# Pinning the spill operations in the gate and up products, and separate buffers for the block sums of the down product

## The chip, the cores and the metric

The kernel runs on one core of one Trainium2 chip. The metric is the time of one execution on the device, in microseconds (us). Engines are named as in the profile: PE is TensorE (PEld its weight load), DVE is VectorE, ACT is ScalarE, POOL is GpSimd, SP is SyncE, which issues most DMAs (SPq is its queue).

## The reference

One step of a streaming encoder layer: RMSNorm, an input projection, two groups of attention heads, an output projection, then the feed-forward part, in which the change lies, and a final RMSNorm.

```
h = rmsnorm(x, lp['norm_ffn_g'])
x = x + (jax.nn.silu(h @ lp['ffn_w_gate']) * (h @ lp['ffn_w_up'])) @ lp['ffn_w_down']
```

There are 576 tokens that are kept (512 prompt and 64 sample), the model width is 2048, the inner width 5632. All data are float32.

## The kernel before

**How a product is made.** The feed-forward part multiplies by blocks in the Winograd form of Strassen's scheme. A weight block of two row tiles by two column tiles has quarters a11, a12, a21, a22; seven products p1 to p7 replace eight. The left operands are p1 = a11, p2 = a12, p4 = a22, p5 = a21 + a22, p6 = (p5's sum) - a11, p3 = a12 - (p6's), p7 = a11 - a21. The tokens, two halves of 288, take the place of the right operand's columns; their combinations are made once and reused.

`winograd` (line 1153) does this for one column block of 256 weights. Its inner function `lhs` (line 1178) makes the left operand of a product: POOL forms p5's sum in a tile `ws` (line 1186) and p7's difference in place in the weights' tile `raw` (line 1195); DVE forms p6's difference in place in `ws` (line 1189) and p3's in place in `raw` (line 1192). `split_weights` then splits the float32 operand in two: ACT copies it, rounded, into `wh` (line 156), and DVE subtracts to get the rest, `wl` (line 153). I call this pair a split. `wh` and `wl` have two buffers each, so the split for one product can be made when PE is done with that of the product before the last. PE multiplies `wh` by both parts of the tokens (line 1207) and then `wl` by the large part (line 1211). `take` then moves the result out of PSUM: in the gate and up products ACT copies (line 1300) and DVE adds (line 1303), in the down product DVE adds into `y` (line 1472). Several products share a PSUM bank and pile up in it; the next one may not start before `take` has read the last.

**Gate and up.** 22 rounds, u = 0 to 21. Each round runs the seven products for the gate weights (I call this a gate set), then the seven for the up weights (an up set), in the order 1, 2, 4, 5, 6, 3, 7. The contraction has 8 steps, so a product is 16 matmuls with `wh` and 8 with `wl`. Behind the gate set `gated` (line 1360) applies the norm's factor on DVE, silu on ACT and the factor again on POOL. Behind the up set POOL multiplies the two (line 1429, two halves) and forms four combinations of the result (lines 1434 to 1437), the right operands of the down product.

**The spill.** These operands don't fit on the chip, so `spill_operands` (line 1340) writes them to memory. It handles two parts of four slices (from u = 20 on one part). Per slice, ACT copies the rounded value to a tile `s` (line 1345) and DVE subtracts it in place from the slice in the tile `c` (line 1346); after four slices two stores of 576 KB go out, and the next part needs the tile `s`, of which there is one, again. The generator is advanced by `step`, which `winograd` calls after each product of the next round: before the change from the second to the sixth product of the gate set and after each of the up set; what is left is run out at the end of the round.

**Who sets the order.** The kernel is written as one program for all engines, and a scheduler orders each engine's instructions. It places an instruction where it takes it to be ready. PE's matmuls are in the order of the program. What the spill does on ACT and DVE may float: the scheduler puts it where it judges the operands to be there. An engine runs its queue in order, so an instruction that waits holds back all behind it.

**Down.** 5632 inner rows are taken in blocks of 4, 4, 4, 4, 4 and 2 pairs of row tiles. For each of the first five blocks there are eight rows of the loop over d (line 1563), each a `winograd` call for 256 output columns (`down_rows`, line 1465) with 4 contraction steps: 8 matmuls with `wh` and 4 with `wl` in a product. I call each of the 40 calls a down row; its products come in the order 1, 5, 6, 2, 7, 3, 4. `raw` has two buffers here, and the weights of a row are loaded by SP when the row before the last has let go of its buffer. The last user of a `raw` is the split of p4. The very first down row still runs beside the spill of u = 21. The block of 2 is multiplied without the scheme (`plain_rows`, line 1445), and `finish` (line 1492) writes the outputs.

`raw` for the first two down rows is loaded by DMAs that POOL issues (line 1402).

Of the kernel before, what the change touches and what calls it, by code (L numbers as in the profile page):

```python
# [19 lines left out]
P = 128  # L20
# [95 lines left out]
def encoder_step(  # L116
# [1034 lines left out]
        return pm.tile([P, 512], F32, name="m", tag="m")  # L1151

    def winograd(wpool, spool, raws, slots, take, banks=None, engine=V, step=lambda: None, stag=("ws", 1),
                 chain=(), made=None):

        first, last = not banks, take is not None
        banks = {} if banks is None else banks

        def split_weights(n, srcs):
            wh = wpool.tile([P, n, P], F32R, name="wh", tag="wh", bufs=2)
            wl = wpool.tile([P, n, P], F32R, name="wl", tag="wl", bufs=2)
            k = 0
            for s in srcs:
                split(wh[:, k:k + s.shape[1], :], wl[:, k:k + s.shape[1], :], s)
                k += s.shape[1]  # L1170
            return wh, wl

        vs = [r.rearrange("p (m t) (f c) -> p t f m c", t=2, f=2) for r in raws]
        n = sum(v.shape[3] for v in vs)
        a11, a12, a21, a22 = ([v[:, t, f] for v in vs] for f in range(2) for t in range(2))
        sums = []

        def lhs(p):
            if made and p in made:
                return made[p]  # L1180
            if p == 5:
                w = spool.tile([P, n, P], F32, name="ws", tag=stag[0], bufs=stag[1])
                ends = np.cumsum([0] + [x.shape[1] for x in a21]).tolist()
                sums.extend(w[:, a:b, :] for a, b in zip(ends, ends[1:]))
                for x, y, z in zip(sums, a21, a22):
                    G.tensor_tensor(x, y, z, op=ALU.add)  # L1186
            elif p == 6:
                for x, y in zip(sums, a11):
                    engine.tensor_tensor(x, x, y, op=ALU.subtract)  # L1189
            elif p == 3:  # L1190
                for x, y in zip(sums, a12):
                    V.tensor_tensor(y, y, x, op=ALU.subtract)
            elif p == 7:
                for x, y in zip(a11, a21):
                    G.tensor_tensor(y, x, y, op=ALU.subtract)  # L1195
            return split_weights(n, {1: a11, 2: a12, 4: a22, 5: sums, 6: sums, 3: a12, 7: a21}[p])

        shared = {}
        for p, name in chain or [(p, p) for p in ORDER]:
            new = name not in shared  # L1200
            if first:
                shared[name] = banks[p] = shared[name] if not new else pmt()[:, 0:QH]
            wh, wl = lhs(p)
            for k in range(n):
                hi, lo = operands[slots[k], p]
                for x in (hi, lo):
                    PE.matmul(banks[p], wh[:, k, :], x, start=first and new and k == 0 and x is hi, stop=False,  # L1207
                              skip_group_check=not new)
            for k in range(n):
                hi, lo = operands[slots[k], p]  # L1210
                PE.matmul(banks[p], wl[:, k, :], hi, start=False, stop=last and k == n - 1,  # L1211
                          skip_group_check=not new)
            if last:
                take(p, banks)
            step()
# [124 lines left out]
    def spill_operands(m, parts):  # L1340

        for first, src in parts:
            hi = squad(F32R)
            for k in range(4):
                S.activation(hi[:, k], src[:, k], AF.Copy)  # L1345
                V.tensor_tensor(src[:, k].bitcast(F32R), src[:, k], f32(hi[:, k]), op=ALU.subtract)  # L1346
                yield
            store(opspill[m, :, first:first + 4, 0], f32(hi))
            store(opspill[m, :, first:first + 4, 1], src)
            yield  # L1350
# [36 lines left out]
    for u in range(FC // 2):  # L1387
        out = {}
        for which, wsrc in (("g", w_gate), ("u", w_up)):
            first = turn == 0  # L1390
            now = raw[:, 0:8] if first else raw
            if turn < FC - 1:
                raw = load_pair((fr, fb)[(turn + 1) % 2], (w_up, w_gate)[turn % 2], (turn + 1) // 2 * 256)
            turn += 1
            c = fc.tile([P, 2, TQ], F32, name="c", tag="c" + which, bufs=1 + (which == "g"))
            chain = () if first else CHAIN if u == FC // 2 - 1 and which == "u" else WIDE
            take = combined(*quarters(c[:, 0, :], c[:, 1, :]), chain)
            if u == FC // 2 - 1 and which == "u":
                raw = fr.tile([P, 16, 256], F32, name="raw", tag="raw", bufs=1)
                fetched = {(0, d): raw[:, 8 * d:8 * d + 8] for d in range(2)}  # L1400
                for d in range(2):
                    G.dma_start(fetched[0, d], w_down[0:1024, d * 256:d * 256 + 256].rearrange("(k p) c -> p k c", p=P))

            products = [0]

            def step():
                products[0] += 1
                if which == "u" or 1 < products[0] < 7:
                    next(spilling, None)
                if u == 0 and which == "u":  # L1410
                    next(norm, None)
                if u == FC // 2 - 1 and which == "u":
                    if products[0] == 2:
                        load_y(0)
                    for _ in range(blocks[0]):
                        next(start, None)

            if first:
                winograd(fw, rw, [now], range(4, 8), take, banks0, step=step)
            else:  # L1420
                winograd(fw, rw, [now], range(8), take, step=step, chain=chain)
            out[which] = c
            if u and which == "g":
                gated(c)
# [40 lines left out]
    def down_rows(m0, n, d, slots, step):  # L1465
        raws = [fetched.pop((m0, d))]
        y11, y12, y21, y22 = quarters(y[2 * d], y[2 * d + 1])
        parts = {1: (y11,), 5: (y22,), 6: (y12,), 2: (y11,), 7: (y22,), 3: (y12,), 4: (y21,)}

        def take(p, banks):  # L1470
            for c in parts[p]:
                V.tensor_tensor(c, c, banks[p], op=ALU.add)  # L1472

        spool, bufs = (yy, 2) if m0 + d else (rw, 1)
        winograd(fw, spool, raws, slots, take, step=step, stag=("ws", bufs), chain=CHAIN)

    tok = [[(0, NS), (NS, P), (192, 96)], [(QH, P), (416, P), (544, 32)]]
    sqs = {}
# [13 lines left out]
    def finish(h, ahead):  # L1492
# [27 lines left out]
        for i, (q, j) in enumerate(groups):  # L1520
            o, n = tok[h][j]
            ps = held.pop(0) if held else turned(q, j)
            tag, bufs = ("ws", 2) if i % 3 < 2 else ("ot", 1)
            ot = yy.tile([P, 4, P], F32, name="ot", tag=tag, bufs=bufs).rearrange("p a b -> p (a b)")
            if i % 2:
                S.activation(ot[0:n], ps[0:n, :], AF.Copy, scale=rc[0:n, j:j + 1])  # L1526
            else:
# [134 lines left out]
```

## Time and profile before

| what | value |
|---|---|
| time, three runs | 2471.19, 2474.02, 2477.39 us; median 2474.02 |
| the profiled execution's own time | 2474.84 us |
| its span | 2473.1 us |
| granted PE clock, mean | 0.995 |
| busy: PE, PEld | 2391.3 us (97%), 2343.1 us (95%) |
| busy: DVE, ACT, POOL | 1856.6 (75%), 1133.8 (46%), 817.1 us (33%) |
| DMA | 353.03 MB, mean 143 GB/s |

The profiled execution took 1.7 us more than its span. Gate and up run from about 907 us to 1915 us of the span, the 40 down rows from there to 2387 us, the rest to the end.

How to read it: a row of a timeline gives the start, the time from the first to the last end of the instructions merged in the row, the engine, line and operation, output and inputs, the count, and in brackets how long the engine stood idle before and what let it go. `PE L1207 ... x16` is the first part of a gate or up product, `L1211 ... x8` its second; in the down rows these are x8 and x4. Ends of matmuls are modelled, so the starts of products tell more than idle times.

### The profile page before, as it was taken

How to read it: one execution, taken by the hardware profiler on the slowest of the kernel's cores; microseconds unless marked ns; L12 is line 12 of the kernel's file. 1: busy time of each engine (PE TensorE's matmuls, PEld its weight loads, DVE VectorE, ACT ScalarE, POOL GpSimd, SP SyncE). 2: the span in 40 equal slices, each digit the busy share in tenths (PEclk: the TensorE clock that was granted, in tenths of full speed). 3: DMA queues.
4: the chain of work that ended last, by engine and by line, in shares of the span. 5: the costliest groups of instructions: out<-in, count | busy, mean ns of one | idle time of the engine just before them, and what ended most of it. 6: DMA issues, size and time to landing. Idle time of an engine off the chain costs nothing. (4 is left out here: it accounts for less than half of the span.)

```text
span 2473.1 us, 44094 instructions
## 1 busy us (share of the span) xinstructions
PE 2391.3 (97%) x17544; PEld 2343.1 (95%) x17544; DVE 1856.6 (75%) x2748; ACT 1133.8 (46%) x1977; POOL 817.1 (33%) x525
## 2 busy tenths in 40 slices
PE   7999999999999999999999999999999999999997
PEld 7999999999998998999999999999999999999986
DVE  5666676666664788778778788787787888888875
ACT  5445545334453554444444444444444333333345
POOL 1100000120000455555555655555554222222245
PEclk9999999999999999999999999999999999999999
DMA  7432233253323644344444444443546873563334
GB/s 223 142 96 83 83 98 94 66 156 102 99 82 118 185 152 146 113 163 151 134 152 141 142 151 134 157 158 113 170 151 212 301 243 125 198 220 108 102 103 145
DMA packets 361972, 353.03 MB, mean 143 GB/s; under 512 B 25087, under 2 KB 319637, under 8 KB 361765
## 3 DMA queue, kind: packets, MB, share of 16 engines
q1 hardware_dynamic: 359535, 343.43, 43.5%
q0 software_dynamic: 1904, 6.24, 0.8%
q8 instruction: 138, 2.26, 0.4%
q10 hardware_dynamic: 325, 0.53, 0.1%
q14 instruction: 70, 0.57, 0.1%
HBM read 271.68 MB, written 81.16 MB: 143 GB/s over the span
## 5 line engine op out<-in xcount | busy, mean ns | idle before, releaser
L1207 PE MATMUL m<-b,wh 128*128 128x288 f32 x7168 | 1050.1, 295 | 16.6 <-DVE y L1472 8.5
L1207 PEld LDWEIGHTS m<-b,wh 128*128 128x128 f32 x7168 | 982.8, 188 | 23.6 <-issue 16.7
L153 DVE TENSOR_TENSOR wl<-raw,wh 128x512 fp32r<-128x512 f32 (+1 forms) x457 | 600.3, 1314 | 59.3 <-ACT wh L156 59.0
L1211 PE MATMUL m<-b,wl 128*128 128x288 f32 x3584 | 583.4, 298 | 11.7 <-DVE wl L153 11.5
L156 ACT ACTIVATE wh<-raw 128x512 fp32r<-128x512 f32 (+1 forms) x457 | 380.1, 832 | 410.3 <-PE m L1207 275.1
L1211 PEld LDWEIGHTS m<-b,wl 128*128 128x128 f32 x3584 | 512.4, 188 | 21.5 <-DVE wl L153 21.5
L1186 POOL TENSOR_TENSOR ws<-raw 128x1024 f32<-128x1024 f32 (+1 forms) x85 | 201.7, 2373 | 619.3 <-DVE wl L153 289.7
L156 ACT ACTIVATE wh<-ws 128x512 fp32r<-128x512 f32 (+1 forms) x170 | 144.2, 848 | 222.3 <-DVE ws L1189 180.0
L108 PE MATMUL ps<-xh,wh 128*128 128x296 f32 x992 | 225.9, 309 | 0.1
L108 PE MATMUL ps<-xl,wh 128*128 128x296 f32 x992 | 217.7, 301 | 0.3 <-DVE xl L161 0.3
L108 PE MATMUL ps<-xh,wl 128*128 128x296 f32 x992 | 216.9, 300 | 0.0
L1195 POOL TENSOR_TENSOR raw<-raw 128x1024 f32<-128x1024 f32 (+1 forms) x85 | 207.1, 2437 | 6.6
L153 DVE TENSOR_TENSOR wl<-ws,wh 128x512 fp32r<-128x512 f32 (+1 forms) x170 | 164.5, 968 | 17.5 <-ACT wh L156 17.4
L1346 DVE TENSOR_TENSOR c<-c,s 128x288 fp32r<-128x288 f32 x168 | 84.6, 533 | 110.6 <-POOL c L1437 59.7
L108 PEld LDWEIGHTS ps<-xh,wh 128*128 128x128 f32 x992 | 161.6, 191 | 3.7 <-issue 0.6
L108 PEld LDWEIGHTS ps<-xl,wh 128*128 128x128 f32 x992 | 162.3, 190 | 1.0 <-DVE xl L161 0.9
L108 PEld LDWEIGHTS ps<-xh,wl 128*128 128x128 f32 x992 | 162.2, 190 | 0.0
L1472 DVE TENSOR_TENSOR y<-y,m 128x288 f32<-128x288 f32 x280 | 126.0, 450 | 46.1 <-PE m L1211 46.1
L153 DVE TENSOR_TENSOR wl<-wr,wh 128x1024 fp32r<-128x1024 f32 (+1 forms) x110 | 120.7, 1097 | 31.7 <-ACT wh L156 30.4
L156 ACT ACTIVATE wh<-wr 128x1024 fp32r<-128x1024 f32 (+1 forms) x110 | 102.2, 929 | 75.3 <-PE ps L108 50.7
L1345 ACT ACTIVATE s<-c 128x288 fp32r<-128x288 f32 x168 | 63.2, 434 | 151.9 <-POOL c L1429 130.6
L1429 POOL TENSOR_TENSOR c<-c 128x576 f32<-128x576 f32 x44 | 101.1, 2297 | 80.6 <-DVE c L1303 78.9
(370 smaller groups left out, 3194.7 us busy)
## 6 DMA issues: line engine op xcount, KB each, us to landing
raw<-in_ffn_w_gate SPq DMA_DIRECT2D x44, 1024.0 KB, 5.5
raw<-in_ffn_w_up SPq DMA_DIRECT2D x44, 1024.0 KB, 7.9
b<-opspill SPq DMA_DIRECT2D x148, 288.0 KB, 5.9
raw<-in_ffn_w_down SPq DMA_DIRECT2D x38, 1024.0 KB, 5.6
wr<-in_w_in SPq DMA_DIRECT2D x56, 512.0 KB, 4.1
opspill<-s SPq DMA_DIRECT2D x42, 576.0 KB, 3.1
opspill<-c SPq DMA_DIRECT2D x42, 576.0 KB, 3.1
wr<-in_w_out SPq DMA_DIRECT2D x16, 512.0 KB, 4.3
```

Source lines behind the costliest of these rows:

```text
L108: self.tc.keep_in_program_order(self.pe.matmul(out, lhsT, rhs, start=start, stop=stop))
L153: V.tensor_tensor(lo, src, f32(hi), op=ALU.subtract)
L156: S.activation(hi, src, AF.Copy)
L1186: G.tensor_tensor(x, y, z, op=ALU.add)
L1195: G.tensor_tensor(y, x, y, op=ALU.subtract)
L1207: PE.matmul(banks[p], wh[:, k, :], x, start=first and new and k == 0 and x is hi, stop=False, skip_group_check=not new)
L1211: PE.matmul(banks[p], wl[:, k, :], hi, start=False, stop=last and k == n - 1, skip_group_check=not new)
L1345: S.activation(hi[:, k], src[:, k], AF.Copy)
L1346: V.tensor_tensor(src[:, k].bitcast(F32R), src[:, k], f32(hi[:, k]), op=ALU.subtract)
L1429: G.tensor_tensor(w[:, f, :], w[:, f, :], g[:, f, :], op=ALU.mult)
L1472: V.tensor_tensor(c, c, banks[p], op=ALU.add)
```

## The change

Three things change.

1. The two spill operations are pinned: `keep_in_program_order` ties an instruction to the one traced just before it on the same engine, so that it can't be placed ahead of that one. It adds no wait. Other instructions may still float. `step` now advances the spill from the third product of a gate set and the second of an up set on.
2. `winograd` gets a switch `within`. For every down row but the first it is off: then p6's and p3's differences on DVE and p7's on POOL go to tiles `ws` of their own instead of being made in place. A row takes four such tiles from three buffers (before: one tile from two buffers). The output tiles of `finish` use the same three buffers, where they had these two and one of their own.
3. The first `raw` of the down product is loaded by SP instead of POOL.

```diff
-                 chain=(), made=None):
+                 chain=(), made=None, within=True):
...
-            if p == 5:
+            if p in (5, 6, 3, 7) and (p == 5 or not within):
                 w = spool.tile([P, n, P], F32, name="ws", tag=stag[0], bufs=stag[1])
                 ends = np.cumsum([0] + [x.shape[1] for x in a21]).tolist()
-                sums.extend(w[:, a:b, :] for a, b in zip(ends, ends[1:]))
-                for x, y, z in zip(sums, a21, a22):
-                    G.tensor_tensor(x, y, z, op=ALU.add)
-            elif p == 6:
-                for x, y in zip(sums, a11):
-                    engine.tensor_tensor(x, x, y, op=ALU.subtract)
-            elif p == 3:
-                for x, y in zip(sums, a12):
-                    V.tensor_tensor(y, y, x, op=ALU.subtract)
-            elif p == 7:
-                for x, y in zip(a11, a21):
-                    G.tensor_tensor(y, x, y, op=ALU.subtract)
-            return split_weights(n, {1: a11, 2: a12, 4: a22, 5: sums, 6: sums, 3: a12, 7: a21}[p])
+                new = [w[:, a:b, :] for a, b in zip(ends, ends[1:])]
+            else:
+                new = {6: sums, 3: a12, 7: a21}.get(p)
+            if p == 5:
+                sums.extend(new)
+            left, right = {5: (a21, a22), 6: (sums, a11), 3: (a12, sums), 7: (a11, a21)}.get(p, ((), ()))
+            for x, y, z in zip(new or (), left, right):
+                (G if p in (5, 7) else V).tensor_tensor(x, y, z, op=ALU.add if p == 5 else ALU.subtract)
+            if p == 6:
+                sums[:] = new
+            return split_weights(n, new or {1: a11, 2: a12, 4: a22}[p])
...
-                S.activation(hi[:, k], src[:, k], AF.Copy)
-                V.tensor_tensor(src[:, k].bitcast(F32R), src[:, k], f32(hi[:, k]), op=ALU.subtract)
+                tc.keep_in_program_order(S.activation(hi[:, k], src[:, k], AF.Copy))
+                tc.keep_in_program_order(
+                    V.tensor_tensor(src[:, k].bitcast(F32R), src[:, k], f32(hi[:, k]), op=ALU.subtract))
...
-                    G.dma_start(fetched[0, d], w_down[0:1024, d * 256:d * 256 + 256].rearrange("(k p) c -> p k c", p=P))
+                    load(fetched[0, d], w_down[0:1024, d * 256:d * 256 + 256].rearrange("(k p) c -> p k c", p=P))
...
-                if which == "u" or 1 < products[0] < 7:
+                if products[0] > (2, 1)[which == "u"]:
                     next(spilling, None)
...
-        spool, bufs = (yy, 2) if m0 + d else (rw, 1)
-        winograd(fw, spool, raws, slots, take, step=step, stag=("ws", bufs), chain=CHAIN)
+        spool, bufs = (yy, 3) if m0 + d else (rw, 1)
+        winograd(fw, spool, raws, slots, take, step=step, stag=("ws", bufs), chain=CHAIN, within=m0 + d == 0)
...
-            tag, bufs = ("ws", 2) if i % 3 < 2 else ("ot", 1)
-            ot = yy.tile([P, 4, P], F32, name="ot", tag=tag, bufs=bufs).rearrange("p a b -> p (a b)")
+            ot = yy.tile([P, 4, P], F32, name="ot", tag="ws", bufs=3).rearrange("p a b -> p (a b)")
```

What this does to the order is shown at two places; line numbers of the changed kernel are one or two smaller from `lhs` on.

The first place is DVE at the border of an up set and the next gate set, in the steady part of gate and up. `wl<-raw` and `wl<-ws` are the second half of a split, `c<-c,m` adds of `take`, `c<-c,s` the spill's subtraction. Before:

```order
L1303 TENSOR_TENSOR c<-c,m 128x288
L153 TENSOR_TENSOR wl<-raw,wh 128x1024
L1346 TENSOR_TENSOR c<-c,s 128x288
L1303 TENSOR_TENSOR c<-c,m 128x288 x2
L153 TENSOR_TENSOR wl<-raw,wh 128x1024
L1346 TENSOR_TENSOR c<-c,s 128x288 x3
L153 TENSOR_TENSOR wl<-raw,wh 128x1024
L1303 TENSOR_TENSOR c<-c,m 128x288
L153 TENSOR_TENSOR wl<-ws,wh 128x1024
```

The three `wl<-raw` are those of the gate set's p1, p2 and p4: one spill subtraction stood ahead of p2's, three ahead of p4's.

The same place now, from p1's `wl` of the gate set on:

```order
L153 TENSOR_TENSOR wl<-raw,wh 128x1024
L1301 TENSOR_TENSOR c<-c,m 128x288 x2
L153 TENSOR_TENSOR wl<-raw,wh 128x1024 x2
L1301 TENSOR_TENSOR c<-c,m 128x288
L153 TENSOR_TENSOR wl<-ws,wh 128x1024
L1191 TENSOR_TENSOR ws<-ws,raw 128x1024
L1191 TENSOR_TENSOR raw<-raw,ws 128x8x128
L153 TENSOR_TENSOR wl<-ws,wh 128x1024
L1345 TENSOR_TENSOR c<-c,s 128x288
L153 TENSOR_TENSOR wl<-raw,wh 128x1024
L1345 TENSOR_TENSOR c<-c,s 128x288
L153 TENSOR_TENSOR wl<-raw,wh 128x1024
```

No spill subtraction stands ahead of p6's `wl` any more; from there on they come one at a time, between splits.

The second place is DVE in a down row, with buffer numbers. Before, the row whose weights are `raw_21432`, from p5's `wl` on; `ws_21748` holds p5's sum and then p6's difference:

```order
L153 TENSOR_TENSOR wl_21751<-ws_21748,wh_21750 128x512
L1189 TENSOR_TENSOR ws_21748<-ws_21748,raw_21432 128x512
L1472 TENSOR_TENSOR y7_21434<-y7_21434,m_21727 128x288
L153 TENSOR_TENSOR wl_21771<-ws_21748,wh_21770 128x512
L1472 TENSOR_TENSOR y7_21434<-y7_21434,m_21747 128x288
L153 TENSOR_TENSOR wl_21791<-raw_21432,wh_21790 128x512
L1192 TENSOR_TENSOR raw_21432<-raw_21432,ws_21748 128x4x128
L1472 TENSOR_TENSOR y7_21434<-y7_21434,m_21727 128x288
L153 TENSOR_TENSOR wl_21811<-raw_21432,wh_21810 128x512
L1472 TENSOR_TENSOR y7_21434<-y7_21434,m_21789 128x288
```

The subtraction for p3 (L1192) stood between the `wl` of p2 and the add that empties p6's bank (the second L1472 on `m_21727`).

The same row now has `raw_21435`; `ws_21757`, `ws_21778`, `ws_21840` and `ws_21819` hold its operands for p5, p6, p3 and p7, and `ws_21906` and `ws_21925` those of the next row, `raw_21584`, for p5 and p6:

```order
L153 TENSOR_TENSOR wl_21760<-ws_21757,wh_21759 128x512
L1191 TENSOR_TENSOR ws_21840<-raw_21435,ws_21778 128x512
L1471 TENSOR_TENSOR y7_21437<-y7_21437,m_21736 128x288
L153 TENSOR_TENSOR wl_21781<-ws_21778,wh_21780 128x512
L1471 TENSOR_TENSOR y7_21437<-y7_21437,m_21756 128x288
L153 TENSOR_TENSOR wl_21801<-raw_21435,wh_21800 128x512
L1471 TENSOR_TENSOR y7_21437<-y7_21437,m_21736 128x288
L153 TENSOR_TENSOR wl_21822<-ws_21819,wh_21821 128x512
L1191 TENSOR_TENSOR ws_21925<-ws_21906,raw_21584 128x512
L1471 TENSOR_TENSOR y7_21437<-y7_21437,m_21799 128x288
L153 TENSOR_TENSOR wl_21843<-ws_21840,wh_21842 128x512
```

The subtraction for p3 has moved up behind p5's `wl`, and p6's for the next row has moved into this one, behind p7's `wl`, so p6's bank is now emptied right after the `wl` of p2.

## The prediction

> **What bounds the kernel now.** I read the page first, then PE's waits, then PE's timeline at those waits, then the queue of the engine that PE waited for.
>
> ```profile
> PE 2391.3 (97%) x17544; PEld 2343.1 (95%) x17544; DVE 1856.6 (75%) x2748; ACT 1133.8 (46%) x1977; POOL 817.1 (33%) x525
> ```
>
> PE is the bound, and nothing in the change touches its work. So the change can only give back what PE loses between products, or make it lose more. Where it loses, by two rows of PE's waits, the first for 980 to 1880 us, the second for the whole span:
>
> ```profile
> PE m L1211 <- DVE wl L153: 8.8, 19, 0.5
> PE m L1207 <- DVE y L1472: 8.5, 7, 1.2
> ```
>
> The first is one wait in every round of gate and up, the second falls in the down rows. PE's timeline in one round shows the full price:
>
> ```profile
> 1302.30 2.28 PE L1207 MATMUL m<-b,wh 128*128 128x288 f32 x16
> ...
> 1327.85 2.28 PE L1207 MATMUL m<-b,wh 128*128 128x288 f32 x16
> 1329.97 1.23 PE L1211 MATMUL m<-b,wl 128*128 128x288 f32 x8
> 1331.04 2.32 PE L1207 MATMUL m<-b,wh 128*128 128x288 f32 x16
> 1333.82 1.34 PE L1211 MATMUL m<-b,wl 128*128 128x288 f32 x8 [0.46 <-DVE wl L153]
> 1334.99 2.28 PE L1207 MATMUL m<-b,wh 128*128 128x288 f32 x16
> ```
>
> From 1302.30 to 1331.04 are nine products, 3.193 us each. The product that waits takes 1334.99 - 1331.04 = 3.95 us. So a wait shown as 0.46 costs 0.76. The second part of a product begins 2.12 us after its start; by then `wl` must be there. DVE and POOL at that place:
>
> ```profile
> 1330.00 0.81 POOL L1437 TENSOR_TENSOR c<-c 128x288 f32<-128x288 f32 x1
> ...
> 1326.63 1.22 DVE L153 TENSOR_TENSOR wl<-raw,wh 128x1024 fp32r<-128x1024 f32 x1
> 1330.84 1.79 DVE L1346 TENSOR_TENSOR c<-c,s 128x288 fp32r<-128x288 f32 x3 [2.99 <-POOL c L1437]
> 1332.56 1.21 DVE L153 TENSOR_TENSOR wl<-raw,wh 128x1024 fp32r<-128x1024 f32 x1
> ```
>
> Three spill subtractions stand ahead of the `wl` of p4 and wait 2.99 us for POOL's combination, which reads the slice they overwrite. That `wl` is then late. The first round with a spill is worse, since POOL is further behind there; ACT, then PE:
>
> ```profile
> 961.01 0.78 ACT L1345 ACTIVATE s<-c 128x288 fp32r<-128x288 f32 x2 [7.25 <-POOL c L1429]
> ...
> 956.99 2.29 PE L1207 MATMUL m<-b,wh 128*128 128x288 f32 x16
> 962.79 2.39 PE L1207 MATMUL m<-b,wh 128*128 128x288 f32 x16 [2.44 <-ACT wh L156]
> 971.30 2.24 PE L1207 MATMUL m<-b,wh 128*128 128x288 f32 x16
> ```
>
> Three products take 14.31 us in place of 9.58: 4.73 lost. How much there is in all, from two windows, u = 1 to 21 and the 40 down rows (the number behind the bounds is the length):
>
> ```profile
> 956.99:1915.06 958.07, 945.33 (x7058) 940.11 (x7057) 760.02 (x755) 449.52 (x669) 518.51 (x253) 1.00 0.46 151
> 1915.06:2386.98 471.92, 459.12 (x3363) 449.16 (x3361) 407.01 (x645) 178.47 (x285) 124.30 (x79) 1.00 0.53 177
> ```
>
> Gate and up: 21 x 14 products x 3.193 = 938.7, so 19.3 us are lost: 4.73 and 19 times 0.76 (14.4), with almost nothing left over. For the down rows I need one that loses nothing:
>
> ```profile
> 2116.62 0.69 DVE L1189 TENSOR_TENSOR ws<-ws,raw 128x512 f32<-128x512 f32 x1
> 2127.77 0.69 DVE L1189 TENSOR_TENSOR ws<-ws,raw 128x512 f32<-128x512 f32 x1
> ```
>
> This row took 11.15 us, 1.593 per product. 40 of them are 446.0, so 25.9 us are lost. A row that loses, on DVE, POOL and PE:
>
> ```profile
> 2082.72 1.77 DVE L153 TENSOR_TENSOR wl<-raw,wh 128x512 fp32r<-128x512 f32 x1
> 2084.53 1.67 DVE L1192 TENSOR_TENSOR raw<-raw,ws 128x512 f32<-128x512 f32 x1
> 2086.12 0.44 DVE L1472 TENSOR_TENSOR y<-y,m 128x288 f32<-128x288 f32 x1
> ...
> 2082.65 1.29 POOL L1186 TENSOR_TENSOR ws<-raw 128x512 f32<-128x512 f32 x1 [8.13 <-ACT wh L156]
> 2084.03 1.63 POOL L1195 TENSOR_TENSOR raw<-raw 128x512 f32<-128x512 f32 x1
> ...
> 2083.75 1.22 PE L1207 MATMUL m<-b,wh 128*128 128x288 f32 x8
> 2086.71 1.30 PE L1207 MATMUL m<-b,wh 128*128 128x288 f32 x8 [1.21 <-DVE y L1472]
> ...
> L1192 DVE TENSOR_TENSOR raw<-raw,ws 128x512 f32<-128x512 f32 x38 | 53.5, 1409 | 1.3
> L1189 DVE TENSOR_TENSOR ws<-ws,raw 128x512 f32<-128x512 f32 x38 | 26.3, 692 | 1.3
> ```
>
> DVE's p2 `wl` and p3 difference each run into one of POOL's two operations and end about 0.55 us after it. Then the add that empties p6's bank comes late, and p7, which goes on in that bank, starts 2.96 us after p2 instead of 1.59. By the groups of 1930 to 2376 us, L1192 takes 1.41 us on average, and L1189 of the same size 0.69.
>
> **The change part by part.** *Pinning.* In the new order the four subtractions of part one stand singly behind the `wl` of p6, p3, p7 and ahead of the next p1. I count time T from the start of p1 of a gate set on PE, which is 1324.66 above (p2 starts at 1327.85). POOL's L1437 ended at 1330.81 and one more of its length follows, so POOL is done with its combinations by T = 7, and the first pinned copy comes behind `take` of p4, after T = 3 x 3.19 = 9.6, so the waits for POOL end. What is late next? Laid out with 1.22 per `wl`, one after the other: `wl` of p5 from 7.0 (behind the add of p2's result), the two differences to 10.7, `wl` of p6 to 11.9, where PE wants it at 12.8 + 2.1 = 14.9. Then POOL's two operations fall in:
>
> ```profile
> 1314.31 2.40 POOL L1186 TENSOR_TENSOR ws<-raw 128x1024 f32<-128x1024 f32 x1 [4.93 <-DVE wl L153]
> 1316.78 3.26 POOL L1195 TENSOR_TENSOR raw<-raw 128x1024 f32<-128x1024 f32 x1
> ...
> 1315.35 2.44 DVE L153 TENSOR_TENSOR wl<-raw,wh 128x1024 fp32r<-128x1024 f32 x1 [1.12 <-ACT wh L156]
> ```
>
> DVE's `wl` waited for POOL's first operation, ended 1.08 us after it, and POOL's second took longer: they take turns. If DVE waits out the first (2.40 from 12.4), `wl` of p3 ends at 15.9 (wanted 18.1); if the subtraction waits out the second, `wl` of p7 ends at 19.7 (wanted 21.3). The smallest slack is 1.6 us. The second part's four subtractions stand between the up set's splits in the same way, its smallest slack is about 2. So I take both losses as gone but for 0 to 2 us: minus 18.3.
>
> The rest of this part is covered. The queue of SP now has a store between the two halves of a gate load:
>
> ```profile
> opspill<-s SPq DMA_DIRECT2D x42, 576.0 KB, 3.1
> raw<-in_ffn_w_up SPq DMA_DIRECT2D x44, 1024.0 KB, 7.9
> raw<-in_ffn_w_down SPq DMA_DIRECT2D x38, 1024.0 KB, 5.6
> ```
>
> It goes out at about T = 21, the second half at 21.5, landing by 30; POOL wants it at 35. The up load stands behind two stores that wait for the up set's last subtraction, goes out at about 44 and lands at 52, which is 7 in the next round; POOL wants it behind the `wl` of p6, at 12. The tile `s` is stored at T = 17, free at 20, wanted at 23. Without these covers each us late would cost a us, 21 times.
>
> *The first down row* shares DVE with the last spill:
>
> ```profile
> 1914.93 0.83 DVE L1346 TENSOR_TENSOR c<-c,s 128x288 fp32r<-128x288 f32 x2 [1.80 <-ACT s L1345]
> ...
> 1925.12 1.22 PE L1207 MATMUL m<-b,wh 128*128 128x288 f32 x8
> ```
>
> Its fifth product starts 10.06 us after 1915.06 instead of 6.37: 3.7 lost. The wait ahead of p5's `wl` goes; POOL's second half of line 1429 still stands against p6's. I take minus 2, bounds 0 and minus 3.7. Moving the first load from POOL to SP is nothing: it isn't wanted until the sum for the first down row.
>
> *Separate buffers.* The other 39 rows lose 25.9 - 3.7 = 22.2 us. Now p3's difference is made behind p5's `wl`, away from POOL's sum, and p7's on POOL waits until the `wl` of p3 has freed its buffer. So p6's bank is emptied right behind p2's `wl`; even if POOL holds that one to 2084.5, the add would end at 2084.9, ahead of 2085.34, when PE wants the bank. That cause goes. What is late next is new: p6's difference for the next row now stands in this row ahead of p3's `wl`, and needs POOL's sum of the next row's weights. Their load waits for p4's `wl` of the row before. This closes a loop of one row, none of it on PE: load 5.6, POOL's sum 1.3, difference 0.7, add 0.4, `wl` of p3 0.7, POOL's p7 1.3, the rest of p4's `wl` 0.55, five signals of about 0.1: 11.05 against 11.15. It is a tie, and a late load decides:
>
> ```profile
> 2008.99 0.38 SPq L137 DMA_DIRECT2D raw<-in_ffn_w_down x1
> 2016.78 1.38 POOL L1186 TENSOR_TENSOR ws<-raw 128x512 f32<-128x512 f32 x1 [10.36 <-DMA raw<-in_ffn_w_down]
> ```
>
> This load took 7.8 us. I take a quarter us per row, 10 of the 22.2 staying, so minus 12; bounds: 0 and minus 22.
>
> The sum is -18.3 - 2 - 12 = -32.3, made against the profiled 2474.84, which is 0.8 above the median. From the median 2474: 2441.
>
> [...]
>
> **The rivals.** A difference of over 0.3% (7.4 us) is what a measurement of this kernel can tell.
>
> - *All losses go*: loads land in time, the loop stays below 11.15. 2474 - 18.3 - 3 - 22 = 2431. For it: most loads land in 5.6. Chance 0.12.
> - *The loop binds*: rows at 11.7. Then 39 x 0.55 = 21 stay, 2474 - 18.3 - 2 - 1 = 2453. For it: loads of 7.8 us exist, and a late row makes the next load late. Chance 0.20.
> - *POOL's lock takes the place of the wait*: in each set the `wl` of p3 waits out both POOL operations instead of one. It is then 0.4 late (18.5 against 18.1), with 0.3 for the restart (0.76 - 0.46), twice a round: 20 x 1.4 = 28 lost where 19.3 are lost now. With the 14 of the down rows it ends at 2474 + 8.7 - 14 = 2469, no change; where it strikes only one set, at 2455. The row at 1315.35 speaks against it, since there the two took turns. 0.04 for 2469, 0.02 for 2455. [...]
> - *Slower*: the loop with late loads. Each us that POOL's sum is late in the loop is a us per row. It is slower by 7.4 from 39 x 1.25 us on, rows of 12.4 us, that is loads of about 7 us in every row: 2482. The median of 5.6 speaks against it. Chance 0.02.
> - That the pins move nothing is excluded by the order shown above.
>
> **How the numbers follow.** My forecast, 2441, has 0.60. Range: 2429 (all 45 us of both windows gone) to 2455 (the loop binds); that leaves out 0.06 of the cases, and about 0.1 more for sizes that are off. Faster: 0.60 + 0.12 + 0.20 + 0.02 = 0.94, same 0.04, slower 0.02.
>
> **What would show it.** Right: no wait of PE for `wl` in gate and up, and rounds of 14 x 3.193 = 44.7 us instead of 45.47; L1471 no longer releases PE in the down rows; DVE or POOL waits for the down loads instead. Wrong: waits of `wl` under POOL's sums in gate sets; down rows at 11.7 or over, with DVE waiting for POOL ahead of p6's difference.

## The result, and the profile after

The changed kernel takes 2442.24 us (median of four runs, 2440.95 to 2442.61); beside it the kernel before took 2474.18. The ratio is 0.9865, with a 95% interval from 0.9852 to 0.9879: faster by 31.9 us, where 33 were forecast (2474 to 2441).

The page's row of busy times after the change:

```profile
PE 2378.6 (97%) x17544; PEld 2340.2 (96%) x17544; DVE 1893.6 (78%) x2748; ACT 1134.1 (46%) x1977; POOL 779.1 (32%) x523
```

PE's matmuls are as many as before. The two windows, from the start of u = 1 to the first down row, and the 40 down rows (the number behind the bounds is the length):

```profile
954.82:1894.38 939.56, 939.31 (x7059) 938.89 (x7057) 805.83 (x754) 449.24 (x669) 499.33 (x251) 1.00 0.47 153
1894.38:2350.87 456.49, 452.77 (x3363) 447.00 (x3361) 398.39 (x645) 178.33 (x285) 104.94 (x79) 1.00 0.55 184
```

Gate and up have come within 0.9 us of the 938.7 that 294 products take without any wait. The down rows have lost 15.4 us, and 10.5 above their 446.0 are left. The down window once more in two parts, the first row and the other 39:

```profile
1894.38:1907.94 13.56, 11.89 (x87) 11.22 (x85) 12.96 (x22) 5.62 (x12) 4.57 (x3) 1.00 1.06 362
1907.94:2350.87 442.93, 440.88 (x3279) 435.78 (x3277) 385.44 (x623) 172.71 (x274) 100.37 (x76) 1.00 0.53 178
```

The same two windows before:

```profile
1915.06:1929.90 14.84, 13.03 (x86) 12.64 (x85) 12.85 (x21) 5.62 (x12) 7.60 (x5) 0.89 1.07 374
1929.90:2386.98 457.08, 446.08 (x3279) 436.52 (x3277) 394.16 (x624) 172.84 (x274) 116.70 (x74) 1.00 0.51 171
```

With these, the span falls apart as follows (us, each from the profiled execution):

| stretch | before | after | difference | forecast |
|---|---|---|---|---|
| start to u = 1 | 956.99 | 954.82 | -2.2 | none |
| gate and up, u = 1 to 21 | 958.07 | 939.56 | -18.5 | -18.3 |
| first down row | 14.84 | 13.56 | -1.3 | -2 |
| other 39 down rows | 457.08 | 442.93 | -14.2 | -12 |
| from there to the end | 86.12 | 89.33 | +3.2 | none |
| span | 2473.1 | 2440.2 | -32.9 | -32.3 |

The two stretches that the prediction left out cancel but for 1 us. Neither can be put down to the change: over the eight experiments below, the first ranges from 954.2 to 958.2 and the last from 85.8 to 88.0, with the old and with the new form of each alike. The 89.33 lies above all of these; 1.7 us of it are a fall of the granted clock (last section).

PE's waits from 980 to 1880 us, where there were 19 of 0.46, are none at all now. In the down rows, `y` of L1471 no longer releases PE. What is left there is seen in one row, on SP, POOL, DVE and PE:

```profile
2087.95 0.38 SPq L137 DMA_DIRECT2D raw<-in_ffn_w_down  x1
...
2099.51 0.38 SPq L137 DMA_DIRECT2D raw<-in_ffn_w_down  x1
...
2094.47 1.30 POOL L1191 TENSOR_TENSOR ws<-raw 128x512 f32<-128x512 f32 x1 [7.13 <-DMA raw<-in_ffn_w_down]
2097.61 1.29 POOL L1191 TENSOR_TENSOR ws<-raw 128x512 f32<-128x512 f32 x1 [1.84 <-DVE wl L153]
...
2095.80 0.69 DVE L1191 TENSOR_TENSOR ws<-ws,raw 128x512 f32<-128x512 f32 x1 [1.18 <-POOL ws L1191]
...
2097.75 1.70 DVE L153 TENSOR_TENSOR wl<-raw,wh 128x512 fp32r<-128x512 f32 x1
...
2098.16 1.22 PE L1205 MATMUL m<-b,wh 128*128 128x288 f32 x8
2099.50 0.80 PE L1209 MATMUL m<-b,wl 128*128 128x288 f32 x4
2100.14 1.22 PE L1205 MATMUL m<-b,wh 128*128 128x288 f32 x8
```

This is the loop that the prediction described. The load goes out at 2087.95; POOL's sum waits for it until 2094.47; p6's difference for the next row waits for the sum and holds DVE; behind it come the `wl` of p3, then POOL's p7, then the `wl` of p4, which runs into POOL's operation and takes 1.70 instead of 0.69 us. PE's p4 lasts 1.98 instead of 1.59 us. When that `wl` is done, the next load goes out at 2099.51: 11.56 after the last one, and a row without a loss is 11.15.

### The profile page after: what moved, and what is told of

It is laid out like the page before. It is cut to its first block, busy times and chain, and to the rows that moved or that the text cites. A ratio compares the mean times of both kernels' runs of the same rounds, so it can differ in the third digit from the quotient of the medians.

```text
span 2440.2 us, 44057 instructions
## 1 busy us (share of the span) xinstructions
PE 2378.6 (97%) x17544; PEld 2340.2 (96%) x17544; DVE 1893.6 (78%) x2748; ACT 1134.1 (46%) x1977; POOL 779.1 (32%) x523
## 5 line engine op out<-in xcount | busy, mean ns | idle before, releaser
L153 DVE TENSOR_TENSOR wl<-raw,wh 128x1024 fp32r<-128x1024 f32 (+1 forms) x379 | 529.9, 1399 | 51.7 <-ACT wh L156 51.4
L156 ACT ACTIVATE wh<-raw 128x1024 fp32r<-128x1024 f32 (+1 forms) x379 | 330.9, 874 | 382.4 <-PE m L1205 322.4
L1191 POOL TENSOR_TENSOR ws<-raw 128x512 f32<-128x512 f32 (+1 forms) x124 | 218.8, 1765 | 605.3 <-DVE wl L153 363.2
L156 ACT ACTIVATE wh<-ws 128x512 fp32r<-128x512 f32 (+1 forms) x248 | 193.4, 780 | 272.8 <-PE m L1205 101.7
L153 DVE TENSOR_TENSOR wl<-ws,wh 128x512 fp32r<-128x512 f32 (+1 forms) x248 | 245.0, 988 | 5.3 <-ACT wh L156 4.5
L1345 DVE TENSOR_TENSOR c<-c,s 128x288 fp32r<-128x288 f32 x168 | 166.5, 991 | 0.0
L1471 DVE TENSOR_TENSOR y<-y,m 128x288 f32<-128x288 f32 x280 | 126.0, 450 | 43.0 <-PE m L1209 42.7
L1191 POOL TENSOR_TENSOR raw<-raw 128x1024 f32<-128x1024 f32 (+1 forms) x46 | 141.9, 3085 | 3.5
L1301 DVE TENSOR_TENSOR c<-c,m 128x288 f32<-128x288 f32 x171 | 73.4, 449 | 88.5 <-PE m L1209 47.6
L1364 POOL TENSOR_TENSOR c<-c,rb 128x576 f32<-128x576 f32 x44 | 79.1, 1797 | 139.0 <-ACT c L1363 139.0
```

The lines of the kernel that those rows point to most:

```text
L153: V.tensor_tensor(lo, src, f32(hi), op=ALU.subtract)
L156: S.activation(hi, src, AF.Copy)
L1191: (G if p in (5, 7) else V).tensor_tensor(x, y, z, op=ALU.add if p == 5 else ALU.subtract)
L1364: G.tensor_tensor(g[:, f, :], g[:, f, :], rb2, op=ALU.mult)
```

## The experiments

All eight were compared with the kernel before on the same chip (2474.26 us there for the first four, 2473.92 for the last four). The stages, from the windows of each profiled execution:

| kernel | time, us (median) | ratio to before, 95% interval | gate and up | first row | other 39 rows |
|---|---|---|---|---|---|
| before | 2474.18 | | 958.07 | 14.84 | 457.08 |
| changed | 2442.24 | 0.9865 (0.9852 to 0.9879) | 939.56 | 13.56 | 442.93 |
| pins only | 2463.72 | 0.9951 (0.9933 to 0.9969) | 943.78 | 15.05 | 458.55 |
| buffers only | 2458.78 | 0.9935 (0.9913 to 0.9957) | 957.74 | 15.11 | 442.81 |
| pins, old `step` | 2459.69 | 0.9939 (0.9917 to 0.9962) | 940.47 | 13.57 | 460.63 |
| changed, load in two tiles | 2431.82 | 0.9824 (0.9797 to 0.9852) | 939.77 | 13.56 | 435.96 |
| changed, load delayed | 2519.77 | 1.0182 (1.0162 to 1.0202) | 939.52 | 13.57 | 517.54 |
| before, load delayed | 2454.23 | 0.9916 (0.9902 to 0.9931) | 958.02 | 13.82 | 439.64 |
| changed, first load by POOL | 2444.76 | 0.9877 (0.9861 to 0.9894) | 943.72 | 14.78 | 442.49 |
| changed, p7 on DVE | 2436.17 | 0.9844 (0.983 to 0.9859) | 939.56 | 12.48 | 437.78 |

**The pins alone.** The kernel before with these lines:

```diff
-                S.activation(hi[:, k], src[:, k], AF.Copy)
-                V.tensor_tensor(src[:, k].bitcast(F32R), src[:, k], f32(hi[:, k]), op=ALU.subtract)
+                tc.keep_in_program_order(S.activation(hi[:, k], src[:, k], AF.Copy))
+                tc.keep_in_program_order(
+                    V.tensor_tensor(src[:, k].bitcast(F32R), src[:, k], f32(hi[:, k]), op=ALU.subtract))
...
-                if which == "u" or 1 < products[0] < 7:
+                if products[0] > (2, 1)[which == "u"]:
```

> The kernel before with the pins and the new rule of step; the down rows and the first load are as before. My theory (the gate and up loss is subtractions that wait for POOL in front of a split, so the order alone cures it): no wait of PE for wl in the steady rounds, the gate and up window 940 instead of 958, the first down row about 1 to 2 us shorter, the other down rows as before with PE still released by the add into y; time 2474 - 18 - 1.5 = 2454. Rival (the separate buffers or the load on SP carry part of the gate and up gain): the window stays above 948 and the time above 2462.

The 19 waits are gone, so the order alone cures the rounds. But the window is 943.8, not 940, and the whole saves 10.5 us, not 20; the single runs spread from 2456.55 to 2469.64. One place in the last up set costs 4.2 us; on PE, ACT, SP and POOL:

```profile
1878.60 2.28 PE L1207 MATMUL m<-b,wh 128*128 128x288 f32 x16
...
1884.42 3.91 PE L1207 MATMUL m<-b,wh 128*128 128x288 f32 x16 [2.46 <-ACT wh L156]
...
1889.23 2.24 PE L1207 MATMUL m<-b,wh 128*128 128x288 f32 x16
...
1883.01 0.41 ACT L1300 ACTIVATE c<-m 128x288 f32<-128x288 f32 x1 [3.91 <-DMA opspill<-c]
...
1873.54 0.37 SPq L140 DMA_DIRECT2D opspill<-c  x1
...
1872.71 1.85 POOL L1403 DMA_DIRECT2D raw<-in_ffn_w_down  x2 [1.75 <-DVE wl L153]
```

ACT's copy into `c` waits for the spill's last store, which still reads that buffer. The store went out at 1873.54 and landed after 9.4 us; the two first down loads, 1 MB each, had gone out on POOL's queue 0.8 us ahead of it. The two products take 10.63 us where 6.39 are needed. My theory did not have this. The rival had named the load on SP as one that may carry part of the gain, and the time lies in its range (above 2462), but the window does not (above 948). Counted back from the start of the first down row, the store goes out 28.4 us ahead of it where it was 39.0 before, and the loads 29.3 where they were 24.9: the pins bring the two together.

**The buffers alone.** The changed kernel with the two spill lines, the rule of `step` and the first load as before.

> The changed kernel with the two spill lines, the rule of step and the first load as before: the separate buffers alone. My theory: the gate and up window stays at 958 with its 19 waits of 0.46, the down rows after the first fall from 457 to about 443, and the end of the program is up to 3 us longer as in the changed kernel; time 2474 - 14 + 2 = 2462. Together with the pins alone the two gains should add up to that of the change (32). Rival (the two parts overlap: the down rows profit because the spill no longer runs into them): the down rows keep most of their loss, time 2470 or more.

PE's waits from 980 to 1870 us are those of before to the digit, and the 39 rows are those of the change (442.81 against 442.93):

```profile
PE m L1209 <- DVE wl L153: 8.8, 19, 0.5
```

So the two parts of the change work apart from each other. The medians give 10.5 us for the pins and 15.5 for the buffers; 26 of 32 together. The third edit, the load on SP, is what neither kernel has: by the run on that load below it is worth 2.5 us in the medians and 4.2 us in the trace of the last up set. The rest of the 6 is not accounted for; the runs of the pins alone spread over 13 us.

**The pins with the old rule of step.** The kernel before with the pinned lines alone.

> The kernel before with the two pins, but the old rule of step (second to sixth product of a gate set, every product of an up set); down rows as before. My theory: what counts is that the subtractions stand singly behind products, since POOL has done its combinations about 7 us into the gate set; the first subtraction now stands ahead of the split of p5, waits about 1 us there, and that split has 4 us to spare. Gate and up window within 2 us of the pins with the new rule (940 to 942), time 2454 to 2456. Rival (the later start is what takes the wait away): PE waits again once a round, window 948 or more, time 2462 or more.

The window is 940.5 with no wait from 980 to 1870 us: pinned, the subtractions stand singly with either rule. Left unpinned, the new rule of `step` gives DVE, ACT and SP exactly the order of before (as the scheduler lays the program out; no such kernel was run), so what counts is the pin. Here the last store goes out at 1871.19, 0.09 us behind the loads on POOL, and lands after 3.8 us, and ACT's copy does not wait for it:

```profile
opspill<-c SPq DMA_DIRECT2D x1, 576.0 KB, 3.8
```

The time is 2459.7 rather than 2455; 3.6 us of that are in the 39 rows, which took 460.6 where they took 457.08 before. Why they did is open.

**The down load in two tiles.** In the changed kernel the weights of a row come as two tiles of 512 KB, left and right columns, each released by itself (the lines that take the quarters from the two tiles are left out):

```diff
...
-            fetched[key] = load_raw(fd, w_down, key[0] * 256, 2 * sizes[key[0]], key[1] * 256, 2)
+            nk, r0 = 2 * sizes[key[0]], key[0] * 256
+            r = [fd.tile([P, nk, P], F32, name=f"raw{f}", tag=f"raw{f}", bufs=2) for f in range(2)]
+            for f in range(2):
+                load(r[f], w_down[r0:r0 + nk * P, key[1] * 256 + f * P:key[1] * 256 + f * P + P].rearrange("(k p) c -> p k c", p=P))
+            fetched[key] = r
```

> The changed kernel, but the weights of a down row come in two tiles of 512 KB, the left columns (a11, a12) and the right columns (a21, a22), each freed and loaded by itself. DVE's order in the rows is the same. Theory of the loop (the last split of a row frees the buffer, the load of 1 MB takes 5.6 us, and the late sum holds DVE and with it POOL's p7 difference and the split of p4): the sum of a21 and a22 starts 1.5 us or more earlier, rows fall to 11.15, the down window from 456.5 to about 449, time 2442 - 7 = 2435. Rival (the loss in the rows is POOL's p7 difference that blocks the split of p4, wherever the load stands): the split of p4 still ends late in most rows, window 455 to 458, time 2441 to 2443.

36 of the 39 rows take 11.15 us. DVE's waits for POOL in the down rows, first of the changed kernel, then of this one (sum, times, longest), and then two rows of POOL's and one of DVE's timeline in this one:

```profile
DVE ws L1191 <- POOL ws L1191: 10.7, 8, 2.0
```

```profile
DVE ws L1192 <- POOL ws L1192: 1.2, 1, 1.2
```

```profile
2111.93 1.29 POOL L1192 TENSOR_TENSOR ws<-raw 128x512 f32<-128x512 f32 x1 [4.92 <-DVE wl L153]
2116.77 1.30 POOL L1192 TENSOR_TENSOR ws<-raw,raw 128x512 f32<-128x512 f32 x1 [3.55 <-issue]
...
2117.38 1.23 DVE L153 TENSOR_TENSOR wl<-raw,wh 128x512 fp32r<-128x512 f32 x1
```

The sum (2111.93) is let go by a buffer, no longer by the load; the loop is open. The sum needs the right columns only. These are still freed by the split of p4, but half as large a load lands after 4.0 us (median) instead of 5.6:

```profile
raw<-in_ffn_w_down SPq DMA_DIRECT2D x76, 512.0 KB, 4.0
```

POOL's p7 (2116.77) still holds up the `wl` of p4, 1.23 us instead of 0.69, but all of it stands earlier in the row and PE does not notice. That excludes the rival. This version beats both kernels: its single runs, 2430.91 to 2432.94, all lie below the lowest of the changed kernel.

**The same delay in both kernels.** Ahead of each load of 1 MB for a down row, its first 128 KB are loaded into the same tile; the load then waits for these:

```diff
         r = pool.tile([P, nk, 256], F32, name="raw", tag=tag, bufs=bufs)
+        if tag == "raw" and nk == 8:
+            start(r[:, 0:1], src[r0:r0 + P, c0:c0 + 256].rearrange("(k p) c -> p k c", p=P))
         start(r, src[r0:r0 + nk * P, c0:c0 + 256].rearrange("(k p) c -> p k c", p=P))
```

> The changed kernel; ahead of each load of 1 MB for a down row from the third on, its first 128 KB are loaded into the same tile, and the load waits until they have landed (2 to 3 us by estimate). The order of DVE in the rows is that of the changed kernel. Theory of the loop: the load stands in a closed loop of one row, of which at most 0.2 us are free, so nearly all of the delay comes back in each row: rows of 13.3 to 14.3 instead of 11.35, time 2442 + 37 x 2 to 3 = 2516 to 2553. Rival (POOL's p7 difference against the split of p4, the load has slack): 2442 to 2446.

> The kernel before with the same delay of its down loads. Theory (before, the rows lose when POOL's sum starts 3.7 to 4.2 us after the row's start on PE and meets the split of p2 and p3's difference; with a start at 4.6 or later they lose nothing): the sum starts 2 to 3 us later, at about 6 or later, rows of 11.15 wherever the load is what the sum waits for: the later load makes the kernel faster, 39 rows from 457 to 435 to 445, time 2474 - 12 to 22 = 2452 to 2462. Rival (late loads are what the rows wait for before, too): rows longer by the delay or by part of it, time above 2480.

In the changed kernel the load goes out 2.42 us later, behind the small one, and DVE's waits for POOL in the down rows grow; from SP's queue, and from DVE's waits:

```profile
2106.67 0.33 SPq L137 DMA_DIRECT2D raw<-in_ffn_w_down  x1
...
2109.09 0.38 SPq L137 DMA_DIRECT2D raw<-in_ffn_w_down  x1
```

```profile
DVE ws L1193 <- POOL ws L1193: 99.9, 35, 5.0
```

The 39 rows grow by 517.54 - 442.93 = 74.6, or 1.91 us each, to 13.27, just under the 13.3 to 14.3 that were expected. DVE's waits for POOL's sum go from 10.7 to 99.9 us. In four rows the scheduler put p6's difference one split later; what became of the other half microsecond of each delay I have not traced.

In the kernel before, the same delay saves 19.7 us: its down window falls from 471.92 to 453.46. Of these 18.5 us, 17.4 are in the 39 rows, and 1.0 is in the first row, which the delay does not touch (more on that row in the next section). Every engine but SP has the order of before. One row there, on POOL and DVE:

```profile
2149.91 1.29 POOL L1188 TENSOR_TENSOR ws<-raw 128x512 f32<-128x512 f32 x1 [6.85 <-DVE wl L153]
2151.28 1.62 POOL L1197 TENSOR_TENSOR raw<-raw 128x512 f32<-128x512 f32 x1
...
2148.19 0.69 DVE L1194 TENSOR_TENSOR raw<-raw,ws 128x512 f32<-128x512 f32 x1
```

POOL's pair now begins behind p3's difference, which takes 0.69 where the mean of before was 1.41. Before, a row lost nothing when the sum began 4.6 us or more after the row's start, 0.6 us at 3.8 to 4.2 and 1.4 us at 3.7; now it begins at 6.1 or later, and a row loses only when the sum ahead of it came at 8.4 or later. So the rows of before did not suffer from late loads but from early ones.

**The first load by POOL.** The changed kernel with one line as before:

```diff
-                    load(fetched[0, d], w_down[0:1024, d * 256:d * 256 + 256].rearrange("(k p) c -> p k c", p=P))
+                    G.dma_start(fetched[0, d], w_down[0:1024, d * 256:d * 256 + 256].rearrange("(k p) c -> p k c", p=P))
```

> The changed kernel with the first two down loads issued by POOL again, as before. My prediction had this at nothing: 2442. What the pins alone showed (the two loads of 1 MB go out 0.8 us ahead of the last spill store of the tile c, which then lands after 9.4 us, and ACT's copy into c waits for it: 4.2 us of PE in the last up set) says 2446, with the stall of PE in the last up set of gate and up and ACT waiting for the store.

The stall is back in the last up set, and so are the 4.2 us (943.72 against 939.56). ACT's copy, waiting for the store, and POOL's two loads:

```profile
1879.81 0.41 ACT L1298 ACTIVATE c<-m 128x288 f32<-128x288 f32 x1 [3.87 <-DMA opspill<-c]
...
1869.56 1.84 POOL L1401 DMA_DIRECT2D raw<-in_ffn_w_down  x2 [1.75 <-DVE wl L153]
```

Of the 4.2 us, 2.6 are the product that waits; 1.6 are the next one, whose 16 matmuls with `wh` take 3.92 us instead of 2.28. With the pins alone they take 3.91, at a granted clock of 0.60 and then 0.55 (last section). PE, DVE and ACT have the same order in both kernels. In the changed kernel, with the load on SP, the same copy waits less, and PE not at all:

```profile
1876.87 0.41 ACT L1298 ACTIVATE c<-m 128x288 f32<-128x288 f32 x1 [1.17 <-DMA opspill<-c]
```

The first down row is 1.2 us longer, too, but that is not shown to come from the load (next section). The medians differ by 2.5 us only, with single runs from 2440.98 to 2447.29, so the trace carries this verdict more than the times do.

**p7's difference on DVE.** In the changed kernel, in the down rows from the second on:

```diff
-                (G if p in (5, 7) else V).tensor_tensor(x, y, z, op=ALU.add if p == 5 else ALU.subtract)
+                (G if p == 5 or (p == 7 and within) else V).tensor_tensor(x, y, z, op=ALU.add if p == 5 else ALU.subtract)
```

> The changed kernel with p7's difference on DVE instead of POOL in the down rows. Theory of the loop: the difference takes 0.7 instead of 1.3 us and the split of p4 no longer waits it out (0.69 instead of 1.70), so the loop is shorter by about 0.6 to 1 us and falls below 11.15: rows 11.15, down window 449, time 2442 - 7 = 2435, though DVE does 0.7 us more in each row. Rival (DVE's work in its row, now about 10.5 us of 11.15, is what bounds): rows of 11.4 or more, time 2442 or above.

The changed row's operations on DVE, p7's difference and the `wl` of p4:

```profile
2105.26 0.69 DVE L1191 TENSOR_TENSOR ws<-raw 128x512 f32<-128x512 f32 x1
...
2106.23 0.69 DVE L153 TENSOR_TENSOR wl<-raw,wh 128x512 fp32r<-128x512 f32 x1
```

The difference (2105.26) takes 0.69 instead of 1.29, and the `wl` of p4 behind it 0.69 instead of 1.70. The rows fall to 437.8, 5.1 less than in the changed kernel, though DVE has an operation more in each. That is 11.23 a row, nearer to the theory's 11.15 than to the rival's 11.4. The first row is 1.1 us shorter, too: a wait of PE for `wl`, 1.07 us in the changed kernel, is gone there.

## Why the prediction was right, and where it was not

**Pinning.** Right in size and in cause: -18.5 against -18.3. The prediction's T begins in this round at 1313.19. The `wl` of p3, laid out to end at T = 15.9, and that of p7, laid out for 19.7, on DVE beside POOL's two operations:

```profile
1325.40 2.56 POOL L1191 TENSOR_TENSOR ws<-raw 128x1024 f32<-128x1024 f32 x1 [4.85 <-DVE wl L153]
1328.04 3.27 POOL L1191 TENSOR_TENSOR raw<-raw 128x1024 f32<-128x1024 f32 x1
...
1326.24 2.80 DVE L153 TENSOR_TENSOR wl<-raw,wh 128x1024 fp32r<-128x1024 f32 x1 [0.55 <-ACT wh L156]
1328.96 2.66 DVE L1345 TENSOR_TENSOR c<-c,s 128x288 fp32r<-128x288 f32 x1
1331.55 1.21 DVE L153 TENSOR_TENSOR wl<-raw,wh 128x1024 fp32r<-128x1024 f32 x1
```

They end at 1329.04 (T = 15.85) and 1332.76 (T = 19.57), ahead of 18.1 and 21.3 when PE wants them. The split takes 2.80 us where the one at 1331.55 takes 1.21, and ends 1.08 us after POOL's sum; the subtraction takes 2.66 where the one at 1332.68 takes 0.45, and ends 0.31 us after POOL's second operation. So each waits out one operation, as assumed, and the rival at 2469, in which the split of p3 waits out both, did not come. Only in the first round with a spill, where POOL is later, does PE wait:

```profile
976.73 1.33 PE L1209 MATMUL m<-b,wl 128*128 128x288 f32 x8 [0.25 <-DVE wl L153]
```

**The first down row.** -1.3 against -2, not by the wait that I named, and for the most part by luck. The row takes 14.8 to 15.1 us in four kernels (before, the pins alone, the buffers alone, the load by POOL), each time at a granted clock of 0.88 or 0.89. It takes 13.6 in the changed one, at 1.00. Its row of the windows with the load by POOL, with the pins and the old `step`, and for before with the load delayed:

```profile
1898.81:1913.59 14.78, 13.21 (x87) 12.75 (x85) 13.17 (x22) 5.63 (x12) 4.57 (x3) 0.88 0.97 331
```

```profile
1895.64:1909.21 13.57, 11.90 (x87) 11.23 (x85) 12.79 (x21) 5.63 (x12) 6.46 (x5) 1.00 1.07 378
```

```profile
1914.23:1928.05 13.82, 11.66 (x86) 11.22 (x85) 12.42 (x21) 5.62 (x12) 5.36 (x4) 1.00 0.89 299
```

In the first of these PE waits as in the changed kernel, 0.49 us for ACT and 1.07 for DVE; it is busy 1.3 us longer for the same work, at the lower clock. That the load does this is not shown: the second kernel also has it on POOL, and its clock stayed. The third waits 1.81 us for ACT, as before does, and its clock stayed, too; its fifth product starts 9.04 us after the first, where the prediction read 10.06 and took all of the 3.7 us lost for waits. So at an equal clock this row goes from 13.82 to 13.56: the wait that I forecast to be worth 2 us was worth 0.3, and the other 1.0 of the 1.3 is a clock that fell in the profile of before and not in that after (more in the last section).

**The load on SP.** This step failed. I put it at nothing because nobody wants the load early. With the pins in and the load on POOL, the last up set loses 4.2 us in two kernels (the pins alone, the load by POOL), 2.6 of it by the wait and 1.6 by the slower product behind it. I had asked who waits for the load, and not which transfer shares the way with it. Before, the loads went out at 1890.13, 14 us behind the spill's last store at 1876.10; in these two kernels the store goes out 0.8 us behind them, and ACT waits for the store. It is a close thing: with the pins and the old `step` the store goes out 0.09 us behind the loads, lands in 3.8 us instead of 9.4, and ACT does not wait for it. The sum came out right because the change moves the load to SP as well: my 18.3 for the pins silently held these 4.2.

**Separate buffers.** -14.2 against -12, by the mechanism given: the add that empties p6's bank is on time, and the loop of one row is what is late next. Which of the three separate tiles does it was not tried one by one; p7's difference on POOL also takes 1.29 us where it was 1.62 in place; that the tile of its own is the cause is not shown. I had put the loop at 11.05 against 11.15 with a quarter us per row for late loads; it measured 442.93 / 39 - 11.15 = 0.21. The rival that the loop binds at 11.7 named the right mechanism, at 0.55 us a row where 0.21 was measured. The price given for it, a us per row for each us that the sum is late, measured 1.91 for a delay of 2.42.

**The rival on the other side**, rows of 12.4 with loads of 7 us, did not come, but its mechanism did when the load was delayed: 2520 us.

## What to carry to other kernels

Before costing a moved transfer at nothing, look at what else is on the DMA engines at its new place, and who waits for that: here a store of 576 KB that somebody waited for landed after 9.4 us, 0.8 us behind two loads that nobody needed yet, and after 3.8 where it went out 0.09 us behind them. When an operation of the next turn is put into this turn of an engine's queue, follow the chain from it back to the last release of its buffer: if it closes, the time of the load is in every turn, as here, where a load delayed by 2.42 us made a row 1.91 us longer. And a later transfer can make a kernel faster, when its arrival triggers work beside which another engine is slower (p3's difference on DVE took 1.41 us on average before, and 0.69 once POOL's pair began behind it): the same 2.4 us of delay took 17 us from the 39 rows of one of these kernels and added 75 to those of the other. Before putting a difference of a stage down to an edit, compare its granted clock in both profiles: a microsecond in the first row came and went with the clock (14.84 us at 0.89, 13.82 at 1.00), while the wait stayed (1.81).

## What the runs showed of the hardware

In these runs a stall of PE cost more than the wait where the granted clock fell behind it, to 0.50 over 2 us at the lowest. The kernel before, in the first down row, where p6 starts 3.57 us after p5; PE's p6, and then 2 us windows, whose third number from the end is the granted clock:

```profile
1920.22 1.80 PE L1207 MATMUL m<-b,wh 128*128 128x288 f32 x8 [1.81 <-ACT wh L156]
```

```profile
1918.00:1920.00 2.00, 0.41 (x4) 0.17 (x2) 2.00 (x3) 1.61 (x4) 1.92 (x2) 1.00 1.05 383
1920.00:1922.00 2.00, 1.78 (x9) 1.63 (x9) 2.00 (x4) 0.00 (x0) 0.89 (x1) 0.69 1.10 354
1922.00:1924.00 2.00, 2.00 (x10) 2.00 (x10) 1.97 (x5) 0.63 (x1) 0.00 (x0) 0.50 1.07 370
1924.00:1926.00 2.00, 2.00 (x16) 2.00 (x16) 1.16 (x5) 0.63 (x1) 1.29 (x1) 0.95 1.08 382
```

The eight matmuls of p6 take 1.80 instead of 1.22 us. The three windows from 1920 us on lack 2 x (0.31 + 0.50 + 0.05) = 1.7 us of clock. In the window of that row, quoted with the result, the clock is 0.89 before and 1.00 after. The same happened behind the stall of the pins alone (0.60 from 1884 to 1886 us, 0.55 from there to 1888), where it makes up 1.6 of the 4.2 us.

Nor does the length of the wait decide it alone. The waits of 0.49 and 1.07 us in the first down row were followed by a fall with the load by POOL and by none in the changed kernel, the wait of 1.81 by one before and by none with the load delayed. Near the end of the program PE waits 1.45 us for ACT before the change and 1.44 after it, at the same place; before, the clock stays at 1.00 behind it, and after the change it falls. The wait before, then that after and the clock behind it:

```profile
2432.24 0.92 PE L189 MATMUL m<-b,wh 128*128 128x288 f32 x3 [1.45 <-ACT wh L156]
```

```profile
2396.67 0.92 PE L189 MATMUL m<-b,wh 128*128 128x288 f32 x3 [1.44 <-ACT wh L156]
```

```profile
2398.00:2400.00 2.00, 2.00 (x13) 2.00 (x12) 1.96 (x6) 1.32 (x2) 0.04 (x1) 0.64 0.43 105
2400.00:2402.00 2.00, 2.00 (x10) 1.90 (x10) 0.57 (x2) 0.26 (x1) 1.81 (x2) 0.51 0.98 335
```

About 1.7 of the 3.2 us by which the end became longer lie here (2 us at 0.64 and 2 at 0.51). What decides whether the clock falls is not shown: it fell behind waits of 1.81, 1.44 and 2.46 us (the last with the pins alone), and in the kernel before it stayed at 1.00 behind one of 2.44 (962.79 us).
